# A two-layer decoder trunk: row blocks 4 to 7 first before the up-projections, attention's low parts on VectorE, and three moves in the order of work

## The chip, the cores and the metric

The kernel runs on one core of a Trainium2 chip. A core has a matrix engine (TensorE, PE in the profile; PEld is its weight load), a vector engine (VectorE, DVE), a scalar engine (ScalarE, ACT), a general engine (GpSimd, POOL) and a sync engine (SyncE, SP) that issues DMAs. They run side by side, each in the order of its own instruction stream, and wait for one another by semaphores. On-chip memory is SBUF; matmul results go to PSUM banks. The metric is the device time of one execution in microseconds (us).

## The reference

A trunk of two layers on one sequence of 1024 rows of 1024 numbers (D). Layer 0 mixes rows by a gated linear recurrence (HGRN2, 8 heads), layer 1 by sliding-window attention (window 128, 16 query heads, 4 key/value heads, a learned sink per head, a relative-position bias). Keys and values are projected once, from layer 0's output. After each mixer and after each feed-forward part stands a layer norm with a weighted residual:

```python
for layer in range(DEPTH):
    if layer < N_A_LAYERS:
        mix = hgrn2_mixer(h, hgrn_w_in[layer], ...)
    else:
        mix = swa_sink_mixer(h, k_shared, v_shared, swa_w_q[j], swa_sinks[j], bias, mask, swa_w_out[j])
    h = layer_norm(ALPHA * h + mix, ln_mix_g[layer], ln_mix_b[layer])
    ff = conv_ffn(h, ffn_w_in[layer], ffn_conv_w[layer], ffn_conv_b[layer], ffn_w_out[layer])
    h = layer_norm(ALPHA * h + ff, ln_ffn_g[layer], ln_ffn_b[layer])
    if layer == N_A_LAYERS - 1:
        k_flat, v_flat = jnp.split(h @ shared_w_kv, 2, axis=-1)

def conv_ffn(h, w_in, conv_w, conv_b, w_out):
    u = h @ w_in                       # 1024 -> 2 * 2816
    u = causal_depthwise_conv(u, conv_w, conv_b)     # width 3
    a, b = jnp.split(u, 2, axis=-1)
    return (jax.nn.silu(a) * b) @ w_out

def swa_sink_mixer(...):
    logits = q k^T * dh**-0.5 + bias, masked to the window
    m = max(logits.max(-1), sink);  p = exp(logits - m)
    return (p v / (p.sum(-1) + exp(sink - m))) @ w_out
```

## The kernel before

**Numbers in two parts.** Each matmul operand is held as a high part (a cast to fp32r by ACT, in `split` and `split_into`, L186 and L141) and a low part, source minus high part (L187 and L142, on VectorE, or on GpSimd where the caller asks for it). `mm3` (L159 to L161) makes one product from three matmuls: high by high, high by low, low by high. So PE can start an operand's product when its high part is there, and needs the low parts one and two matmuls later.

**Places.** T holds the transposed activations (both parts), Y the row blocks (8 blocks tb of 128 rows), HL is twelve weight tiles; a pair of them is a slot (`hl_at(i)`, six slots), given out in turn by `ring["hl"]`. `psmm` has four PSUM banks, `psax` two of twice the size.

**Order.** PE's order is that of the program text everywhere; in attention (from the `with tc.manual_schedule` near the end) the order of ACT, VectorE and GpSimd is that of the text too. Elsewhere a scheduler orders the other engines by priority, which follows the text. `Order` (od) is a planner by which chains of small work are put into the text between matmuls: a generator is spawned, yields a waiting time (in us of PE time that the planner counts), and is continued by `od.tick()` when this has passed, or by `od.finish()` at once. Loads go out from SP's queue in the order of its stream.

**Output projection and up-projection** (`out_proj`, `Up`). For each column half dh and each row block tb the projection's product is added to the residual (L321), and half of the norm's statistics taken (L200). In the second half the chain `Up.ln` starts for the block: `ln_normal` (statistics L206, L207, power on GpSimd L208, then the normalisation on VectorE L222 for blocks 0 to 3 or on ACT L218 for blocks 4 to 7), a store of the normal rows (L353), a yield of 8.0, `ln_turn` (eight transposes L169, then the norm's scale and shift out of PSUM, L234 on ACT or L236 on VectorE), and the split into T. The up-projection is done with Strassen-like sums: seven products per group fc of columns (`product`), of which 1 and 2 read rows 0 to 511 of T, 4 and 5 rows 512 to 1023, and 6, 7 and 3 sums of both halves, made by L365 to L369 and held in TX. `weights(fc)` loads a group's weights into the tiles rx and splits them (`weight_load`), then makes sums of them (`weight_sums`, L404 to L407): products 1 and 2 need plain weights, 4 and 5 summed ones. `run` starts with products 1 and 2 of two groups in psax banks, while the chains of blocks 4 to 7 end, then takes products 4 and 5 in psmm banks, and so on.

**From layer 0 to attention.** The down-projection's last evacuations (L578) end blocks 4 to 7. Each block's `ln_mid` normalises, yields 11.0 or 8.0, turns the block through psax banks (two of four columns each on VectorE, L236) and splits it to T. Around these chains PE runs `k_part(0)` (keys of rows 0 to 511; low part Kl on VectorE, L1058), three `v_part`s, `k_part(1)` and the first query projection. Key weights lie in slots 0 and 1, value weights in 2 and 3. `ln_rows` multiplies the normal rows of all eight blocks by the norm's gain (VectorE, L251), adds its shift (GpSimd, L252) and stores them as layer 1's residual; it starts after block 7's chain, during `k_part(1)`.

**Attention.** Eight query groups c, in each four steps bp. A step runs stages of four steps at once: scores (L1119, L1122), copy and mask (L1124 to L1131), bias on GpSimd (L1134), maximum and sink (L1139, L1142, L1143), exponential, division (L1150 to L1152), transposes, triangle mask (L1160), output (L1165 and on), and between them a quarter of the next group's query projection (`q_proj`, `q_split` L1107). Weights of the group after next (`q_unit`) and of the output projection (`out_unit`) and the move of the output from Y to T (`Y_to_T`, steps 26 to 31) have their low parts on GpSimd.

## Time and profile before

| | us |
|---|---|
| median of 3 runs (2301.88 to 2304.33) | 2304.32 |
| profiled execution | 2307.7 |
| its span | 2305.9 |
| PE busy in the span | 2225.4 (97%) |
| DVE busy | 1878.7 (81%) |
| ACT busy | 916.5 (40%) |
| POOL busy | 282.1 (12%) |

The span goes from the first to the last instruction of the profiled execution. Rows of a timeline give start and duration in us, engine, line, operation, tiles and shapes, and in square brackets the idle time before it with what ended it. Rows of a group give busy time and mean duration in ns. A granted clock of 1.00 is TensorE at full speed.

### The profile page before, as it was taken

Reading aid. Unit: us, or ns where it says so; the run is one execution under the profiler, and the core shown is the slowest. Engines: PE = TensorE matmul, PEld = TensorE weight load, DVE = VectorE, ACT = ScalarE, POOL = GpSimd, SP = SyncE. Lnnn points to the kernel's source line nnn. Section 1 sums busy time; section 2 is a strip of 40 time slices with the busy share of each in tenths; the row PEclk is TensorE's granted clock in tenths of the full one; section 3 lists DMA queues with packets and bytes.
Section 4 is the critical chain, followed back from the end, with each engine's and each line's share of the span. In section 5 each row is a group of like instructions: output and inputs, shape, how many; then the busy total and the mean of one; then the engine's idle time right before and its main releaser. Section 6 shows DMA issues by size and latency. Waiting matters only on the chain.

```text
span 2305.9 us, 30677 instructions
## 1 busy us (share of the span) xinstructions
PE 2225.4 (97%) x11743; PEld 1862.0 (81%) x11743; DVE 1878.7 (81%) x2413; ACT 916.5 (40%) x1553; POOL 282.1 (12%) x246
## 2 busy tenths in 40 slices
PE   8999999999989999999999899989999999999998
PEld 7788889888878888888788687767788888887887
DVE  3688887655769988888997658996689888889987
ACT  4122122232555444444343435653744444443431
POOL 0223222221000000000000063450100000000001
PEclk9999999999999999999999999989999999999999
DMA  6355454312312322226955331113212222238663
GB/s 213 39 183 201 165 185 148 95 39 92 110 46 92 101 83 83 83 82 208 306 166 172 93 101 26 41 56 101 92 55 92 92 83 82 83 125 293 217 216 140
DMA packets 231932, 281.32 MB, mean 122 GB/s; under 512 B 29977, under 2 KB 160618, under 8 KB 228970
## 3 DMA queue, kind: packets, MB, share of 16 engines
q1 hardware_dynamic: 228898, 276.92, 36.7%
q10 hardware_dynamic: 2888, 2.45, 0.8%
q8 instruction: 92, 1.51, 0.3%
q14 instruction: 54, 0.44, 0.1%
HBM read 214.31 MB, written 65.01 MB: 121 GB/s over the span
## 4 chain that ended last, share of the span: by engine, by line
PE 70%; DVE 16%; DMA 6%; ACT 4%; issue 3%; POOL 1%; SPq 0%; DVEq 0%; ACTq 0%; POOLq 0%
PE psmm L159 13%; PE psmm L161 13%; PE psmm L160 13%; PE psax L159 8%; PE psax L161 8%; PE psax L160 8%; PE psax L165 4%; DMA raw<-in_hgrn_w_in_dram 2%; DVE T L187 1%; DMA bsd<-Y 1%; ACT Y L234 1%; DVE Y L452 1%; PE psmm L165 1%; DMA Y<-in_ffn_w_out_dram 1%; DVE A L805 1%
## 5 line engine op out<-in xcount | busy, mean ns | idle before, releaser
L159 PE MATMUL psmm<-T,HL 128*128 128x512 f32 x768 | 311.4, 406 | 5.6 <-ACT T L186 5.6
L160 PE MATMUL psmm<-T,HL 128*128 128x512 f32 x768 | 303.8, 396 | 4.9 <-DVE T L187 4.9
L161 PE MATMUL psmm<-T,HL 128*128 128x512 f32 x768 | 304.3, 396 | 4.0 <-DVE HL L142 4.0
L452 DVE SCALAR_TENSOR_TENSOR Y<-Y,cwt 128x1023 f32<-128x1023 f32 (+1 forms) x176 | 225.0, 1279 | 40.6 <-ACT Y L450 40.3
L450 ACT ACTIVATE Y<-Y,cwt 128x1024 f32<-128x1024 f32 x88 | 108.9, 1238 | 269.2 <-DVE Y L439 265.1
L159 PE MATMUL psmm<-HL,T 128*128 128x256 f32 (+1 forms) x656 | 199.3, 304 | 1.8 <-issue 1.4
L161 PE MATMUL psmm<-HL,T 128*128 128x256 f32 (+1 forms) x656 | 195.6, 298 | 1.0 <-DVE T L187 1.0
L160 PE MATMUL psmm<-HL,T 128*128 128x256 f32 (+1 forms) x656 | 195.6, 298 | 0.6 <-DVE HL L142 0.6
L208 POOL TENSOR_TENSOR rs<-rs,nhalf 128x1 f32<-128x1 f32 x32 | 26.4, 826 | 1375.8 <-DVE rs L207 1375.6
L186 ACT CAST HL<-rx 128x1024 fp32r<-128x1024 f32 (+1 forms) x137 | 140.3, 1045 | 130.6 <-DMA rx<-in_ffn_w_in_dram 44.8
L161 PEld LDWEIGHTS psmm<-T,HL 128*128 128x128 f32 x768 | 146.6, 191 | 36.8 <-DVE HL L142 4.5
L187 DVE TENSOR_TENSOR HL<-rx,HL 128x1024 fp32r<-128x1024 f32 (+1 forms) x137 | 165.2, 1210 | 13.5 <-ACT HL L186 13.2
L159 PEld LDWEIGHTS psmm<-T,HL 128*128 128x128 f32 x768 | 147.0, 191 | 36.0 <-ACT T L186 6.5
L160 PEld LDWEIGHTS psmm<-T,HL 128*128 128x128 f32 x768 | 146.9, 191 | 34.3 <-DVE T L187 5.5
L159 PE MATMUL psax<-T,HL 128*128 128x512 f32 x352 | 137.9, 392 | 0.0
L161 PE MATMUL psax<-T,HL 128*128 128x512 f32 x352 | 137.4, 390 | 0.0
L160 PE MATMUL psax<-T,HL 128*128 128x512 f32 x352 | 137.1, 389 | 0.0
L159 PEld LDWEIGHTS psmm<-HL,T 128*128 128x128 f32 x656 | 126.8, 193 | 5.7 <-issue 1.6
L160 PEld LDWEIGHTS psmm<-HL,T 128*128 128x128 f32 x656 | 126.6, 193 | 4.5 <-DVE HL L142 0.9
L161 PEld LDWEIGHTS psmm<-HL,T 128*128 128x128 f32 x656 | 126.2, 192 | 4.6 <-DVE T L187 1.2
L825 POOL TENSOR_TENSOR kp<-kp,tot 128x512 f32<-128x512 f32 x48 | 69.3, 1443 | 216.8 <-PE psax L165 182.9
L186 ACT CAST HT<-rx 128x1024 fp32r<-128x1024 f32 (+1 forms) x51 | 43.9, 861 | 95.8 <-PE psmm L160 30.1
(301 smaller groups left out, 5547.4 us busy)
## 6 DMA issues: line engine op xcount, KB each, us to landing
rx<-in_ffn_w_in_dram SPq DMA_DIRECT2D x136, 256.0 KB, 3.4
rx<-gd SPq DMA_DIRECT2D x118, 256.0 KB, 3.4
Y<-in_ffn_w_out_dram SPq DMA_DIRECT2D x44, 512.0 KB, 3.7
bsd<-Y SPq DMA_DIRECT2D x22, 1024.0 KB, 7.2
gd<-Y SPq DMA_DIRECT2D x44, 512.0 KB, 2.7
rx<-in_ffn_w_out_dram SPq DMA_DIRECT2D x54, 256.0 KB, 3.9
R<-bsd SPq DMA_DIRECT2D x44, 256.0 KB, 4.4
Y<-in_ffn_w_in_dram SPq DMA_DIRECT2D x40, 256.0 KB, 3.0
```

Of the source, the lines that this page charges most:

```text
L159: nc.tensor.matmul(ps, st(0), mv(0), start=start, stop=False)
L160: nc.tensor.matmul(ps, st(0), mv(1), start=False, stop=False)
L161: nc.tensor.matmul(ps, st(1), mv(0), start=False, stop=stop)
L165: nc.tensor.matmul(ps, lhsT, rhs, start=start, stop=stop, **kw)
L186: nc.scalar.copy(hi, src)
L187: return (eng or nc.vector).tensor_tensor(lo, src, hi.bitcast(F32), op=ALU.subtract)
L208: nc.gpsimd.tensor_tensor(rs, rs, nhalf, op=ALU.pow)
L234: nc.scalar.activation(hf[:, kc, :], ps[:, k * P:(k + 1) * P], AF.Identity, bias=shift, scale=scale)
L450: nc.scalar.activation(c, u, AF.Identity, bias=cwt[:, l, 3, ci:ci + 1], scale=cwt[:, l, 2, ci:ci + 1])
L452: nc.vector.scalar_tensor_tensor(c[:, sh:], u[:, :S - sh], cwt[:, l, 2 - sh, ci:ci + 1], c[:, sh:], op0=ALU.mult, op1=ALU.add)
L805: nc.vector.copy_predicated(dst, mask.unsqueeze(1).to_broadcast(list(dst.shape)), src)
L825: nc.gpsimd.tensor_tensor(kv[:, :, 0, :], kv[:, :, 0, :], tv[:, :, 1:2].to_broadcast([P, nb, m]), op=ALU.mult)
```

## The change

Five parts:

- `out_proj` takes the row blocks of its second column half in the order 4, 5, 6, 7, 0, 1, 2, 3. The up-projection begins with products 4 and 5 of two groups (psax banks); when the last chains are done, products 1 and 2 follow in psmm banks. Sums of both halves are now made in the chains of blocks 0 to 3. Blocks 2 and 3 are turned into rx[1] and rx[2].
- `urgent()`, a raised priority for the scheduler, stands around the evacuation and the norm's chain in `out_proj` and `Up.ln`.
- Key weights go to slots 4 and 5, value weights to 0 and 1; query and output weights get slots from a written list.
- `ln_mid` waits 9.0 instead of 8.0 for blocks 4 to 7 and turns a block in two halves with a yield of 1.2 between them. `ln_rows` runs in two batches: blocks 0 to 3 are spawned before `k_part(0)`, blocks 4 to 7 where all eight were.
- The low parts of query weights, output weights and `Y_to_T` go to a list, `lows`, and are issued on VectorE: late in each attention step, after `q_split`, and for the first two query units right after their casts.

```diff
@@ -120,6 +120,10 @@
     def psax():
         return axp.tile([P, 1024], F32, name="psax")
 
+    def urgent():
+
+        return tc.high_priority(offset=300)
+
 
     ring = {"hl": 4, "raw": 0}
     tail, place = {}, {}
@@ -137,9 +141,17 @@
             nc.sync.dma_start(view, src)
         return raw
 
+    def low_part(lo, src, hi, eng):
+
+        make = lambda e: e.tensor_tensor(lo, src, hi.bitcast(F32), op=ALU.subtract)
+        if isinstance(eng, list):
+            eng.append(lambda: make(nc.vector))
+        else:
+            return make(eng or nc.vector)
+
     def split_into(hl, raw, eng=None):
         nc.scalar.copy(hl[:, 0], raw)
-        (eng or nc.vector).tensor_tensor(hl[:, 1], raw, hl[:, 0].bitcast(F32), op=ALU.subtract)
+        low_part(hl[:, 1], raw, hl[:, 0], eng)
         return hl
 
     def split_raw(raw, eng=None):
@@ -184,7 +196,7 @@
 
     def split(hi, lo, src, eng=None):
         nc.scalar.copy(hi, src)
-        return (eng or nc.vector).tensor_tensor(lo, src, hi.bitcast(F32), op=ALU.subtract)
+        return low_part(lo, src, hi, eng)
 
     def split_scaled(hi, lo, src, scale):
         nc.scalar.activation(hi, src, AF.Copy, scale=scale)
@@ -221,9 +233,9 @@
             yq = y[:, q * 512:(q + 1) * 512]
             nc.vector.tensor_scalar(yq, yq, mv[:, 0:1], rs, op0=ALU.subtract, op1=ALU.mult)
 
-    def ln_turn(tb, hf, gcol, bcol, banks, on_vector=0):
-
-        for q in range(2):
+    def ln_turn(tb, hf, gcol, bcol, banks, on_vector=0, halves=range(2)):
+
+        for q in halves:
             ps = banks(q)
             for k in range(4):
                 tr(ps[:, k * P:(k + 1) * P], Y[:, tb, (4 * q + k) * P:(4 * q + k + 1) * P])
@@ -238,20 +250,22 @@
 
     def ln_mid(tb, gcol, bcol):
         ln_normal(tb)
-        yield 11.0 if tb < 4 else 8.0
+        yield 11.0 if tb < 4 else 9.0
         hf = place["hf"](tb)
-        ln_turn(tb, hf, gcol, bcol, lambda q: psax()[:, :512], 2)
+        for q in range(2):
+            ln_turn(tb, hf, gcol, bcol, lambda _: psax()[:, :512], 2, (q,))
+            if q == 0:
+                yield 1.2
         ts = slice(tb * P, (tb + 1) * P)
         split(T[:, 0, :, ts], T[:, 1, :, ts], hf)
 
-    def ln_rows(rows, wait, spill=None):
-        for tb in range(NB):
+    def ln_rows(tbs, rows, wait, spill):
+        for tb in tbs:
             for h in range(2):
                 y = Y[:, tb, h * 512:(h + 1) * 512]
                 nc.vector.tensor_tensor(y, y, rows[0][h], op=ALU.mult)
                 nc.gpsimd.tensor_tensor(y, y, rows[1][h], op=ALU.add)
-            if spill is not None:
-                nc.sync.dma_start(spill[:, tb, :], Y[:, tb, :])
+            nc.sync.dma_start(spill[:, tb, :], Y[:, tb, :])
             yield wait
 
     def ln_last(tb, rows):
@@ -312,14 +326,17 @@
                     out_late(late, rows, tb, ff.TX)
                 elif dh == 0 and tb == 4:
                     ff.weights(0)
+                if dh:
+                    tb = (tb + 4) % NB
                 if dh == 0 and tb < len(begun):
                     ps = begun[tb]
                 else:
                     ps = psmm()
                     out_part(ps, late if dh else us, tb, range(KC))
                 y = Y[:, tb, dh * 512:(dh + 1) * 512]
-                nc.vector.scalar_tensor_tensor(y, y, ALPHA, ps, op0=ALU.mult, op1=ALU.add)
-                ln_half(tb, dh)
+                with urgent() if dh else nullcontext():
+                    nc.vector.scalar_tensor_tensor(y, y, ALPHA, ps, op0=ALU.mult, op1=ALU.add)
+                    ln_half(tb, dh)
                 if dh == 1:
                     tasks.append(od.spawn(ln(tb)))
                     od.tick()
@@ -349,28 +366,31 @@
             self.W, self.raw, self.pieces = {}, {}, 0
 
         def ln(self, tb, gcol, bcol):
-            ln_normal(tb, tb > 3)
-            nc.sync.dma_start(ynd[:, tb, :], Y[:, tb, :])
+            with urgent():
+                ln_normal(tb, tb > 3)
+                nc.sync.dma_start(ynd[:, tb, :], Y[:, tb, :])
             yield 8.0
-            turned = lambda t: (self.rx[2] if t == NB - 1 else Y[:, t, :]).rearrange("p (k t) -> p k t", k=KC)
+            turned = lambda t: (self.rx[t - 1] if t in (2, 3) else Y[:, t, :]).rearrange("p (k t) -> p k t", k=KC)
             hf = turned(tb)
-            ln_turn(tb, hf, gcol, bcol, lambda q: psmm())
             ts = slice(tb * P, (tb + 1) * P)
-            if tb < 4:
+            with urgent():
+                ln_turn(tb, hf, gcol, bcol, lambda q: psmm())
+                if tb > 3:
+                    a21, a22 = hf[:, :4], hf[:, 4:]
+                    split(T[:, 0, 4:, ts], T[:, 1, 4:, ts], a22)
+                    tt(a22, a21, a22, op=add)
+                    split(T[:, 0, :4, ts], T[:, 1, :4, ts], a22)
+                    return
                 split(T[:, 0, :, ts], T[:, 1, :, ts], hf)
-                return
-            pf, xs = turned(tb - 4), slice((tb - 4) * P, (tb - 3) * P)
-            a11, a12, a21, a22 = pf[:, :4], pf[:, 4:], hf[:, :4], hf[:, 4:]
-            split(T[:, 0, 4:, ts], T[:, 1, 4:, ts], a22)
-            tt(a22, a21, a22, op=add)
-            split(T[:, 0, :4, ts], T[:, 1, :4, ts], a22)
+            sf = turned(tb + 4)
+            a11, a12, a21, s1 = hf[:, :4], hf[:, 4:], sf[:, :4], sf[:, 4:]
             tt(a21, a11, a21, op=sub)
-            tt(a11, a22, a11, op=sub)
+            tt(a11, s1, a11, op=sub)
             tt(a12, a12, a11, op=sub)
-            split(self.TX[:, 2, 0, :, xs], self.TX[:, 2, 1, :, xs], a21)
+            split(self.TX[:, 2, 0, :, ts], self.TX[:, 2, 1, :, ts], a21)
             yield 100.0
-            pair = pf.rearrange("p (c k) t -> p c k t", c=2)
-            split(self.TX[:, :2, 0, :, xs], self.TX[:, :2, 1, :, xs], pair)
+            pair = hf.rearrange("p (c k) t -> p c k t", c=2)
+            split(self.TX[:, :2, 0, :, ts], self.TX[:, :2, 1, :, ts], pair)
 
         def weights(self, fc):
             self.weight_load(fc)
@@ -458,26 +478,24 @@
                     nc.sync.dma_start(gd[:, fc, :], ca)
 
         def run(self, ready, down):
+
             od.finish(ready[:4])
             tiles = [psax(), psax()]
             ax = [tiles[i % 2][:, i // 2 * 512:(i // 2 + 1) * 512] for i in range(4)]
-            first = [(p, fc) for fc in range(2) for p in (1, 2)]
-            for (p, fc), ps in zip(first, ax):
+
+            for (p, fc), ps in zip([(p, fc) for p in (4, 5) for fc in range(2)], ax):
                 self.product(p, fc, ps)
             od.finish(ready[4:])
             mm = [psmm() for _ in range(4)]
             self.pairs = [mm, ax]
-            for (p, fc), ps in zip(first, ax):
-                self.collect(p, fc, ps)
-
-            for n, (p, fc) in enumerate([(p, fc) for p in (4, 5) for fc in range(2)]):
-                self.product(p, fc, mm[n])
+            for (p, fc), ps in zip([(p, fc) for p in (1, 2) for fc in range(2)], mm):
+                self.collect(p, fc, self.product(p, fc, ps))
             for fc in range(2):
-                self.collect(6, fc, self.product(6, fc, ax[fc]))
+                self.collect(6, fc, self.product(6, fc, mm[fc]))
             for fc in range(2):
-                self.collect(7, fc, self.product(7, fc, ax[2 + fc]))
-                self.collect(4, fc, mm[fc])
-                self.collect(5, fc, mm[2 + fc])
+                self.collect(7, fc, self.product(7, fc, mm[2 + fc]))
+                self.collect(4, fc, ax[fc])
+                self.collect(5, fc, ax[2 + fc])
             self.weight_load(2)
             for fc in range(2):
                 self.product(3, fc, mm[fc])
@@ -1038,14 +1056,14 @@
         Vt = at.tile([P, NB, 256], F32, name="Vt")
         khl, uv = [], []
         for c in range(2):
-            hl = split_into(hl_at(c), load(lambda r: [(r.rearrange("p (k c) -> p k c", k=KC),
+            hl = split_into(hl_at(4 + c), load(lambda r: [(r.rearrange("p (k c) -> p k c", k=KC),
                                                        wkvv[:, :, c * P:(c + 1) * P])]))
             khl.append(hl.rearrange("p h (k c) -> p h k c", k=KC))
         for u in range(2):
-            hl = split_into(hl_at(2 + u), load(lambda r: [(r.rearrange("p (k c) -> p k c", k=4),
+            hl = split_into(hl_at(u), load(lambda r: [(r.rearrange("p (k c) -> p k c", k=4),
                                                            wkvv[:, 4 * u:4 * u + 4, 256:512])]))
             uv.append(hl.rearrange("p h (k c) -> p h k c", k=4))
-        ring["hl"] = 4
+
         def k_part(half):
             ts = slice(half * 512, (half + 1) * 512)
             for c in range(2):
@@ -1077,11 +1095,14 @@
             nc.sync.dma_start(bfs[c], bass.AP(tensor=rbd.tensor, offset=rbd.offset + (8 * pp + r) * 2 * P * P + P - 1,
                                               ap=[[2 * P - 1, P], [8 * P * P, 2], [1, P]]))
 
+        lows = []
+
         def q_unit(c):
             bias_load(c)
             pp, r = divmod(c, 4)
+            ring["hl"] = (2, 3, 4, 5, 0, 1, 4, 5)[c]
             hl = unit(lambda t: [(t.rearrange("p (k g e) -> p k g e", k=KC, g=2)[:, :, g, :],
-                                  wq[:, :, 8 * pp + 4 * g + r, :]) for g in range(2)], nc.gpsimd)
+                                  wq[:, :, 8 * pp + 4 * g + r, :]) for g in range(2)], lows)
             return hl.rearrange("p h (k c) -> p h k c", k=KC)
 
         def q_proj(hl):
@@ -1204,25 +1225,32 @@
             out_part(begun[1], us, 1, [6])
             yield
 
+        def make_lows():
+            while lows:
+                lows.pop(0)()
+
         flight = []
         with tc.manual_schedule(engines={EN.PE, EN.Activation, EN.DVE, EN.Pool}):
             od.finish(lns[:4])
+            late = [od.spawn(ln_rows(range(4), rows, 2.0, h2d))]
             k_part(0)
             for tp in range(3):
                 od.finish(lns[2 * tp:2 * tp + 2])
                 v_part(tp)
             od.finish(lns[6:])
             hl = q_unit(0)
-            late = od.spawn(ln_rows(rows, 2.0, h2d))
+            make_lows()
+            late.append(od.spawn(ln_rows(range(4, NB), rows, 2.0, h2d)))
             k_part(1)
             g = q_proj(hl)
             q, done = next(g)
             hl = q_unit(1)
+            make_lows()
             for _ in g:
                 while done:
                     q_split(*done.pop(0))
                 od.tick()
-            od.finish([late])
+            od.finish(late)
             nc.scalar.activation(sm.tile([P, 1], F32, name="warm"), nhalf, AF.Exp)
             us = []
             moves = {26: (0, 3, 0, 4), 27: (3, 6, 0, 4), 28: (0, 3, 4, 8), 29: (3, 6, 4, 8),
@@ -1235,7 +1263,7 @@
                     it = attend(c, bp, q)
                     prev = [None] * (3 - len(flight)) + flight
                     if 4 * c + bp in moves:
-                        Y_to_T(*moves[4 * c + bp], nc.gpsimd)
+                        Y_to_T(*moves[4 * c + bp], lows)
                     stage(it)
                     stage(prev[0])
                     stage(prev[2])
@@ -1246,6 +1274,7 @@
                     stage(prev[2])
                     while done:
                         q_split(*done.pop(0))
+                    make_lows()
                     if bp == 0 and c < 6:
                         hl = q_unit(c + 2)
                     stage(fill)
@@ -1256,7 +1285,8 @@
                     if c == 0 and bp == 1:
                         v_part(3)
                     if 0 <= 4 * c + bp - 21 < 4:
-                        us.extend(out_unit(rows2, 4 * c + bp - 21, nc.gpsimd))
+                        ring["hl"] = 4 * c + bp - 21
+                        us.extend(out_unit(rows2, 4 * c + bp - 21, lows))
                     flight.append(it)
                 q = nq
             a29, a30, a31 = flight
```

2 lines of the change are left out of this document (1 added, 1 removed).

## The prediction

> **What bounds the kernel now.** I read the busy times first, then windows over the stretches where TensorE (PE) has gaps, then PE's waits there, and last the timelines of the engine that ended each wait.
>
> ```profile
> span 2305.9 us, 30677 instructions
> ## 1 busy us (share of the span) xinstructions
> PE 2225.4 (97%) x11743; PEld 1862.0 (81%) x11743; DVE 1878.7 (81%) x2413; ACT 916.5 (40%) x1553; POOL 282.1 (12%) x246
> ```
>
> PE is busy 97%, and the change leaves its matmuls what they are. So only PE's idle time, 2305.9 − 2225.4 = 80.5 us, and stretches at a lowered clock can be won, or added to. The profiled run took 2307.7 us, 3.4 above the median of 2304.32; I sum against it and carry the difference over to the median.
>
> ```profile
> 643.50:663.50 20.00, 14.12 (x68) 10.81 (x67) 16.75 (x28) 18.28 (x38) 2.23 (x5) 0.98 0.22 79
> 663.50:677.20 13.70, 13.70 (x49) 11.04 (x50) 10.66 (x14) 5.22 (x8) 0.00 (x0) 0.79 0.13 38
> 1296.50:1321.00 24.50, 17.55 (x83) 13.28 (x82) 17.89 (x33) 11.87 (x21) 1.10 (x2) 0.93 0.40 86
> 1378.50:1384.00 5.50, 5.43 (x20) 4.28 (x21) 4.69 (x11) 2.82 (x11) 1.49 (x2) 0.69 0.06 9
> 1400.00:1500.00 100.00, 99.74 (x695) 78.79 (x694) 88.38 (x177) 61.07 (x218) 41.03 (x48) 1.00 0.15 38
> 1501.80:1564.50 62.70, 51.70 (x324) 39.61 (x323) 57.83 (x95) 34.70 (x111) 36.14 (x24) 0.89 0.17 59
> ```
>
> Columns: window, length, busy time of PE, weight load, VectorE (DVE), ScalarE (ACT) and GpSimd (POOL), granted clock, DMA share, GB/s. In attention's middle (1400 to 1500) PE is full. It is not in four places that the change touches: the start of each up-projection (A), the hand-over from layer 0 to the key projection (B), attention's start (C) and its end (D).
>
> **A: the first products, both layers.** Before, products 1 and 2 run on row blocks 0 to 3, and product 4 then waits for block 7.
>
> ```profile
> 653.20 1.03 PE L169 MATMUL psmm<-ident,Y 128*128 128x128 f32 x8
> ...
> 660.37 0.50 PE L159 MATMUL psmm<-T,HL 128*128 128x512 f32 x1 [2.70 <-ACT T L186]
> 663.30 0.80 PE L160 MATMUL psmm<-T,HL 128*128 128x512 f32 x1 [2.43 <-DVE T L187]
> ```
> ```profile
> 1667.64 0.50 PE L159 MATMUL psmm<-T,HL 128*128 128x512 f32 x1 [2.94 <-ACT T L186]
> 1670.57 0.80 PE L160 MATMUL psmm<-T,HL 128*128 128x512 f32 x1 [2.43 <-DVE T L187]
> ```
> ```profile
> 654.91 1.05 ACT L186 CAST HL<-rx 128x1024 fp32r<-128x1024 f32 x1
> 655.85 0.64 ACT L186 CAST T<-Y 128x512 fp32r<-128x512 f32 x1
> 656.37 2.92 ACT L234 ACTIVATE rx<-psmm,par 128x128 f32<-128x128 f32 x8
> 659.12 0.68 ACT L186 CAST T<-Y 128x512 fp32r<-128x512 f32 x1
> 659.63 0.69 ACT L186 CAST T<-rx 128x512 fp32r<-128x512 f32 x1
> ```
> ```profile
> 661.36 0.68 DVE L187 TENSOR_TENSOR TX<-Y,TX 128x512 fp32r<-128x512 f32 x1
> 661.96 0.68 DVE L369 TENSOR_TENSOR Y<-Y 128x512 f32<-128x512 f32 x1
> 662.56 0.68 DVE L187 TENSOR_TENSOR T<-rx,T 128x512 fp32r<-128x512 f32 x1
> ```
>
> Block 7's turn on ACT begins at 656.37, three microseconds behind its transposes, since a weight cast (HL<-rx) and block 6's cast stand ahead of it and it needs rx[2], which that cast has to read first. Its low part stands behind sums of block 6 (TX, L369). The idle is 2.70 + 2.43 = 5.1 us, and the clock behind it falls to 0.79 over 13.7 us, 0.21 × 13.7 = 2.9 us: 8.0 in layer 0; in layer 1, 2.94 + 2.43 and as much clock, 8.3.
>
> After, blocks 4 to 7 come first in the second column half, products 4 and 5 run on them, and products 1 and 2 wait for block 3, whose chain now ends last. Products 4 and 5 need the weight sums of both first groups; these stand on DVE some 20 us ahead of the products in the new order. I keep the end of block 3's transposes at block 7's (653.20, first rows just after). Its eight turns take 2.92 and no longer wait for rx[2] (block 3 goes to rx[2] too, which the weight sums, now earlier, have left by then), so they end near 656; one cast of 1024 columns at 1.05 and one low part (below, 1.22) follow, to 657.3 and 658.4. PE comes off products 4 and 5 when it came off the first products, at 660.37 − 2.70 = 657.7, or up to 0.8 earlier: waits of about 0.4 and 0.9 us, and I add 0.8 of clock, 2.1 in all. The gain is 5.9 and 6.2, **−12.1**. It is at least 3.5 (should the TX cast and two sums get ahead of it, 1.6 + 2 × 0.68 a layer, with the whole clock loss kept) and at most 16.3, all of it. The loads that are moved (the next weights' on SP's queue behind the products, four 128 KB pieces) are due after some 20 us; sums pushed back by the urgent evacuations are due at product 6, four products later, which take the 13.7 us of the second window. I cost both at nothing; without that cover product 6 would wait by one pair of sums, 1.4 us.
>
> **B: layer 0's end, key projection.**
>
> ```profile
> PE psmm L161 <- DVE HL L142: 4.0, 1, 4.0
> PE psax L169 <- DVE q L236: 2.6, 2, 2.3
> PE psax L169 <- issue: 0.3, 1, 0.3
> ```
> ```profile
> L236 DVE TENSOR_SCALAR q<-psax,par 128x128 f32<-128x128 f32 x16 | 5.6, 404 | 1.5 <-ACT q L234 1.5
> L1058 DVE TENSOR_TENSOR Kl<-psmm,Kh 64x512 fp32r<-64x512 f32 x8 | 5.5, 687 | 18.0 <-ACT Kh L1057 17.9
> L187 DVE TENSOR_TENSOR T<-q,T 128x1024 fp32r<-128x1024 f32 x4 | 4.9, 1225 | 4.7 <-ACT T L186 4.7
> L142 DVE TENSOR_TENSOR HL<-raw,HL 128x1024 fp32r<-128x1024 f32 x4 | 4.8, 1216 | 0.3 <-ACT HL L141 0.3
> ```
> ```profile
> 1288.61 0.69 DVE L578 TENSOR_TENSOR Y<-Y,psmm 128x512 f32<-128x512 f32 x1 [6.62 <-PE psmm L161]
> ```
> ```profile
> L251 DVE TENSOR_TENSOR Y<-Y,X 128x512 f32<-128x512 f32 x16 | 18.0, 1185 | 0.1
> ```
>
> (PE's waits from 1296 to 1322; groups from 1296 to 1580, the last two numbers before the bar being busy us and mean ns.) The key weights' slots 0 and 1 come free only with the down-projection's end, hence the wait of 4.0 us for their low part. In slots 4 and 5 the two low parts (2 × 1.22) fit into DVE's idle 6.62 us before 1288.61, so the 4.0 go. Against it stands the first batch of residual rows: eight multiplications on DVE, 8 × 1.185 = 9.5 us, each followed by an addition on POOL, put between the norm of blocks 4 to 7 and the turns (L236) that release PE's two transpose banks. DVE's window has 17.89 of 24.5 busy; without the four lows and with the rows it is 17.89 − 4.8 + 9.5 = 22.6, and PE can run ahead of nothing: it owns two banks, and the turn in two halves makes it come back for each. Placing the instructions in the new order by these durations, PE stalls 5.4 us for the first turn (behind block 7's norm and the first pair of rows), 1.7 and 2.3 at the next, and 6.2 behind a low part, Kl's four casts and more rows: 15.6 in place of 4.0 + 2.6 + 0.3 = 6.9, with 1.2 less of clock lost. **+7.5**; from −3 (rows hidden in the free 6.6 us) to +11 (all 9.5 uncovered, and one more turn). The four stores of residual rows move up SP's queue with them, ahead of the query weights' loads; those are due some 20 us later.
>
> **C: attention's start.**
>
> ```profile
> 1361.52 0.33 PE L1119 MATMUL psax<-Kh,q 128*128 128x128 f32 x1 [1.02 <-DVE q L1107]
> ```
> ```profile
> 1378.57 0.63 PE L169 MATMUL psmm<-ident,X 128*128 128x128 f32 x4 [1.45 <-DVE X L1152]
> ```
> ```profile
> 1358.82 12.25 POOL L252 TENSOR_TENSOR Y<-Y,X 128x512 f32<-128x512 f32 x8
> ```
>
> POOL's backlog of rows lasts until 1371 and holds up the first bias additions; PE idles 1.02 and 1.45 and then runs at 0.69 for 5.5 us (1.7): 4.2 us. With half of the rows gone and the low parts of two query units on DVE I leave 0.4: **−3.8** (0 if those lows delay DVE as much; −5 at best).
>
> The Trainium skill (TensorE: Matmul & The Clock Gate, "Why this matters for your kernels") asks for no PE gaps over some 3 us, since one idle window lowers the clock. The trace differs: the gap of 1.45 us has a clock of 0.69 right behind it. By the page the small waits left in A would cost no clock, and the sum would be 1.6 us lower; I go by the trace.
>
> **D: attention's end.**
>
> ```profile
> 1529.67 0.16 DVE L1142 SCALAR_TENSOR_TENSOR nm<-nm,nsk 128x4 f32<-128x4 f32 x1
> 1529.87 3.39 DVE L1143 TENSOR_TENSOR se<-sk,nm 128x4 f32<-128x4 f32 x1
> ```
> ```profile
> 1529.79 3.45 POOL L187 TENSOR_TENSOR T<-Y,T 128x1536 fp32r<-128x1536 f32 x1 [3.90 <-ACT T L186]
> ```
>
> A DVE instruction on four columns takes 3.39 us, as long as the POOL low part beside it, where its like took 0.16: DVE stands still while POOL reads. In the window PE idles 62.7 − 51.7 = 11.0 us and loses 0.11 × 51.7 = 5.7 to the clock: 16.7. After, the lows are DVE's own: five of 1.22, four 1536 wide at 1.5 × 1.22 = 1.83, two 512 wide at 0.68, 14.8 us in eleven steps, put last in each step, where nothing of that step waits behind them. Bounds: all hidden but for DVE's leftover share, 11.6% of 62.7 = 7.3, would leave 14.8 − 7.3 = 7.5 if that share is all there is, none if the freed stalls count too (−13 after some lost clock); nothing hidden leaves 14.8 (−2). I leave 8.0, near the row of the free share: **−8.7**. The casts stand a step ahead of the lows, so DVE does not wait for them.
>
> The Trainium skill (SBUF — State Buffer, "Who interferes with whom") says that a DVE instruction with two SBUF inputs and a GpSimd instruction that reads SBUF lock each other out wholly. The rows of D agree, and it speaks against B, where such pairs are moved into the norm's window; the mean of 1185 ns has that lock in it.
>
> **Sum:** −12.1 + 7.5 − 3.8 − 8.7 = −17.1: 2307.7 − 17.1 = 2290.6 for the profiled run, 2304.3 − 17.1 = **2287** for the median.
>
> **Rivals.** (1) B is hidden: rows fit into DVE's gaps and the 4.0 is won. For it: DVE's 6.6 free us; against: two banks only. 2304.3 − 12.1 − 3 − 3.8 − 8.7 = 2277. (2) A brings nothing: block 3 ends as late against PE as block 7 did, for the same casts and sums still stand on ACT and DVE, and the urgent order moves only some. Against: one cast of 1024 replaces two steps and a sum. 2304.3 + 7.5 − 3.8 − 8.7 = 2299. (3) Slower: DVE becomes attention's bound. If none of its free time can be used and the stalls remain for another reason, the lows of all attention, 12 × 1.22 + 4 × 1.83 + 2 × 0.68 = 23.3 us, are added with none of D won: 2304.3 − 12.1 + 7.5 − 3.8 + 23.3 = 2319. It decides once attention gets longer by 8.4 us. For it: DVE at 88.38% while PE is full; against: that share includes its standing still beside POOL.
>
> **How the numbers follow.** Likeliest 0.54, around 2287 (2280 to 2296 by itself); (1) 0.17; (2) 0.15, about half of it within 0.2% (4.6 us, about what can be told from no change); (3) 0.14, a tenth of it inside that bound. Faster is 0.54 + 0.17 + 0.08 = 0.79, same 0.08, slower 0.13. The range takes in (1) and (2): 2274 to 2301, and leaves out (3) and the tail under (1).
>
> **What would show it.** Right: PE's waits for T at the first products under 1 us each, with the clock above 0.9 behind them; no wait for HL in the first key matmul; L236 late and longer PE waits on psax from 1300 to 1330; L1142 and L1143 at 0.16 throughout, steps of the last two query groups between 5.6 and 6.8 us. Wrong: the wait at product 1 as long as product 4's was; attention's middle with PE below 97 of 100 us; or a new wait on slots of HL.

## The result and the profile after

The changed kernel takes 2293.71 us (median of 5 runs, 2293.41 to 2294.85), the kernel before 2304.33 beside it: a ratio of 0.9951, 95% interval 0.9937 to 0.9966, 10.6 us less. The forecast was 2287, 17.1 us less.

The page after, and a table of windows over the four places (length, busy time of PE, weight load, DVE, ACT and POOL, granted clock, DMA share, GB/s): the first products of layer 0 (A), the hand-over to the key projection (B), attention's start (C) and its end (D).

```profile
span 2291.7 us, 30675 instructions
...
PE 2221.3 (97%) x11743; PEld 1861.2 (81%) x11743; DVE 1866.8 (81%) x2431; ACT 917.0 (40%) x1553; POOL 237.0 (10%) x228
```
```profile
657.00:675.00 18.00, 15.08 (x59) 11.71 (x58) 10.59 (x14) 7.81 (x10) 0.00 (x0) 0.91 0.30 87
1293.00:1328.00 35.00, 22.38 (x101) 18.12 (x100) 26.04 (x44) 13.79 (x26) 13.03 (x10) 0.80 0.34 96
1364.00:1372.00 8.00, 7.43 (x36) 5.50 (x35) 3.65 (x9) 5.42 (x9) 1.88 (x4) 1.00 0.31 66
1497.00:1549.50 52.50, 50.20 (x334) 38.98 (x333) 48.11 (x95) 35.33 (x106) 12.86 (x14) 0.97 0.19 62
```

The window of D is now 52.5 us long with PE busy for 50.2 of them, where it was 62.7 with 51.7 (334 PE instructions against 324). B has become the worst place: 35 us with 22.4 busy, at a clock of 0.80. DVE has the low parts and yet less busy time in the span than before (1866.8 against 1878.7): in attention's last steps it no longer stands still beside GpSimd.

Every trace holds the same 11743 PE instructions (matmuls and transposes), so a stretch can be taken between the same two PE instructions, counted in PE's order, in two traces. The table gives how much longer (+) or shorter (−) each stretch is than in the first profile of before, in us: A0 and A1 the up-projections' starts in layers 0 and 1 (593.7 to 735.8 and 1640.6 to 1761.1 before), B 1284.1 to 1323.9, C 1343.0 to 1399.5, D 1486.5 to 1598.6, and the rest of the span. The times are medians; the ratio is to the kernel before, run beside it on the same chip.

| run | A0 | B | C | D | A1 | rest | us | ratio, interval |
|---|---|---|---|---|---|---|---|---|
| changed | −5.5 | +8.3 | −3.8 | −10.4 | −4.1 | +1.3 | 2293.71 | 0.9951, 0.9937 to 0.9966 |
| before_again | −1.0 | +1.0 | −1.6 | 0.0 | +0.3 | +2.0 | 2306.82 | 1.0001, 0.9989 to 1.0013 |
| rows_once | −5.5 | +3.6 | +4.0 | −10.4 | −5.9 | +4.2 | 2295.51 | 0.9961, 0.9946 to 0.9976 |
| turn_whole | −4.8 | +3.8 | −3.8 | −10.4 | −4.0 | +2.2 | 2290.60 | 0.9931, 0.9910 to 0.9951 |
| rows_once_whole | −4.1 | −2.9 | +4.1 | −10.4 | −5.8 | +8.4 | 2290.88 | 0.9936, 0.9915 to 0.9956 |
| pool_lows | −4.5 | +8.9 | −3.8 | 0.0 | −4.3 | +1.3 | 2304.26 | 0.9998, 0.9988 to 1.0007 |
| order_back | +0.5 | +9.3 | −3.8 | −10.2 | −0.1 | −2.0 | 2301.14 | 0.9984, 0.9974 to 0.9993 |
| slots_back | −5.3 | +11.4 | −3.8 | −10.4 | −3.9 | +3.5 | 2298.11 | 0.9959, 0.9942 to 0.9977 |
| cast_half | −9.1 | +7.7 | −3.8 | −10.4 | −8.2 | +3.5 | 2286.86 | 0.9910, 0.9893 to 0.9927 |
| rows_v_whole | −4.3 | +6.1 | −3.7 | −10.4 | −3.2 | +2.0 | 2294.21 | 0.9942, 0.9926 to 0.9959 |
| best | −9.2 | +6.2 | −3.3 | −10.3 | −7.7 | +3.4 | 2287.25 | 0.9914, 0.9894 to 0.9935 |
| best2 | −8.7 | −5.7 | +3.2 | −10.3 | −7.9 | +5.6 | 2279.75 | 0.9884, 0.9866 to 0.9903 |
| best3 | −8.7 | −6.3 | +7.4 | −10.3 | −8.1 | +0.8 | 2283.64 | 0.9902, 0.9885 to 0.9920 |

The rest holds little that was changed: attention's middle, 1399.5 to 1486.5, where low parts moved too, is 0.4 us shorter in every run but pool_lows and before_again. Yet the rest goes from −2 to +8 us from profile to profile. Most of that lies in the first 165 us, where every engine has the same instructions in the same order in all fourteen traces, and which still take from 0.6 us less to 5.6 us more than in the first profile. So a time says less of a part than the stretch that the part touches. Stretches that a run leaves alone repeat better: D within 0.2 us, C within 0.1 but for the two profiles of before, B from +7.7 to +9.3, A1 from −3.2 to −5.9. The last section shows that the lowered clock comes in steps of some 1.7 us, and A1 had none, one or two of them.

### The profile page after: what moved, and what is told of

Read it like the earlier page. It is cut to its first block, busy times and chain, and to the rows that moved or that the text cites. A ratio compares the mean times of both kernels' runs of the same rounds, so it can differ in the third digit from the quotient of the medians.

```text
span 2291.7 us, 30675 instructions
## 1 busy us (share of the span) xinstructions
PE 2221.3 (97%) x11743; PEld 1861.2 (81%) x11743; DVE 1866.8 (81%) x2431; ACT 917.0 (40%) x1553; POOL 237.0 (10%) x228
## 5 line engine op out<-in xcount | busy, mean ns | idle before, releaser
L146 DVE TENSOR_TENSOR HL<-raw,HL 128x1024 fp32r<-128x1024 f32 x51 | 66.9, 1314 | 48.2 <-ACT HL L153 48.1
```

The lines of the kernel that those rows point to most:

```text
L146: make = lambda e: e.tensor_tensor(lo, src, hi.bitcast(F32), op=ALU.subtract)
```

## The experiments

**The kernel before once more.** 

> The kernel before, once more, for a second profile. If the 3.4 us by which its first profile was longer than the median of its runs lie in stretches that the change does not touch (the first 600 us), the stretches of this profile differ from the first by 1 to 3 us there and by less than 0.5 us from the first up-projection on; then the gain of the four places is taken from them, and not from the difference of the two profiled times. If they lie in the four places, the gains read there were too large.

The second profile has stretches from the first up-projection on that differ by up to 1.6 us, not by less than 0.5, and its run is again longer than its median (2308.55 against 2306.82). In the four places, first and second profile differ by just over 1 us in sum. So the gains read from the table are good to one or two microseconds each; the sum of the changed kernel's places, −15.5, and the measured −10.6 are not reconciled by it.

**Attention's low parts back on GpSimd.**

```diff
-for g in range(2)], lows)                      # q_unit
+for g in range(2)], lows if c < 2 else nc.gpsimd)
-Y_to_T(*moves[4 * c + bp], lows)
+Y_to_T(*moves[4 * c + bp], nc.gpsimd)
-us.extend(out_unit(rows2, 4 * c + bp - 21, lows))
+us.extend(out_unit(rows2, 4 * c + bp - 21, nc.gpsimd))
```

> Low parts of attention's steps back on GpSimd (the first two query units' stay on VectorE), all else as changed. Theory: attention's last eleven steps lost their time to VectorE standing still beside GpSimd's low parts; its small instructions take 1.6 to 3.4 us again there, the stretch is about 10.9 us longer, 2304 us. Rival: the new order of slots and the later place of the lows did it; then within 2 us of 2294.

D is back at 0.0, 10.4 us longer than in the changed kernel, at 2304.26. Groups of DVE from attention's part of each trace (the last two numbers before the bar are busy us and mean ns), first of this run, then of the changed kernel:

```profile
L1163 DVE SCALAR_TENSOR_TENSOR nm<-nm,nsk 128x4 f32<-128x4 f32 x32 | 26.0, 811 | 1.1
```
```profile
L1163 DVE SCALAR_TENSOR_TENSOR nm<-nm,nsk 128x4 f32<-128x4 f32 x32 | 5.2, 162 | 1.1
```

The same four-column instruction takes 0.81 us on average with the low parts on GpSimd and 0.16 without: over 32 of them 21 us of DVE. A timeline of DVE in this run shows that it is not one operation's doing: here this instruction takes 0.17 us and the next, also of four columns, 3.37, as in the kernel before. GpSimd's low part of 1536 columns runs beside it:

```profile
1530.53 0.17 DVE L1163 SCALAR_TENSOR_TENSOR nm<-nm,nsk 128x4 f32<-128x4 f32 x1
1530.73 3.37 DVE L1164 TENSOR_TENSOR se<-sk,nm 128x4 f32<-128x4 f32 x1
```
```profile
1530.64 3.45 POOL L146 TENSOR_TENSOR T<-Y,T 128x1536 fp32r<-128x1536 f32 x1 [3.89 <-ACT T L198]
```

That D's gain comes from taking the low parts off GpSimd, and not from the slots, is shown. This run also gives up their later place in the step, and no run puts them at another place on DVE; what the place is worth by itself is not shown.

**The row blocks' order back.**

```diff
-                if dh:
-                    tb = (tb + 4) % NB
...
-            for (p, fc), ps in zip([(p, fc) for p in (4, 5) for fc in range(2)], ax):
+            first = [(p, fc) for fc in range(2) for p in (1, 2)]
+            for (p, fc), ps in zip(first, ax):
```

(and the bodies of `Up.ln` and `run` that go with it, with `urgent()` kept)

> Row blocks in the order 0 to 7 and products 1 and 2 first as before, the raised priority and all else as changed. Theory: the order won the 5.5 and 3.7 us at the two up-projections, so both come back: PE waits for block 7's T by 2.7 + 2.4 us again, 2303 us. Rival: the raised priority alone won them: waits under 3.5 us in sum per layer, 2294 to 2297 us.

A0 and A1 are at +0.5 and −0.1: without the order (and the places of blocks 2 and 3 that belong to it), the raised priority wins nothing that shows, and the time is 2301.14. PE's timeline in this run:

```profile
662.48 0.62 PE L171 MATMUL psmm<-T,HL 128*128 128x512 f32 x1 [3.56 <-ACT T L198]
663.69 0.80 PE L172 MATMUL psmm<-T,HL 128*128 128x512 f32 x1 [0.60 <-DVE T L146]
```

The waits came in another division than expected (3.6 + 0.6, not 2.7 + 2.4), with two shorter ones, 0.39 and 1.54 us for the norm on ACT, ahead of them.

**What is left at the first products.** PE, ACT and DVE of the changed kernel at layer 0's first product, and PE in layer 1:

```profile
659.87 0.51 PE L171 MATMUL psmm<-T,HL 128*128 128x512 f32 x1 [2.17 <-ACT T L198]
661.13 0.69 PE L172 MATMUL psmm<-T,HL 128*128 128x512 f32 x1 [0.75 <-DVE T L146]
```
```profile
1656.94 0.50 PE L171 MATMUL psmm<-T,HL 128*128 128x512 f32 x1 [2.17 <-ACT T L198]
1658.20 0.80 PE L172 MATMUL psmm<-T,HL 128*128 128x512 f32 x1 [0.76 <-DVE T L146]
```
```profile
658.25 0.62 ACT L198 CAST TX<-Y 128x512 fp32r<-128x512 f32 x1 [1.37 <-DVE Y L387]
658.78 1.04 ACT L198 CAST T<-rx 128x1024 fp32r<-128x1024 f32 x1
```
```profile
656.21 0.68 DVE L388 TENSOR_TENSOR rx<-Y,rx 128x512 f32<-128x512 f32 x1
656.93 0.69 DVE L389 TENSOR_TENSOR rx<-rx 128x512 f32<-128x512 f32 x1
657.54 0.68 DVE L387 TENSOR_TENSOR Y<-rx,Y 128x512 f32<-128x512 f32 x1
```

Block 3's cast to T was ready when its turn ended (1.37 us before 658.25), but stands on ACT behind a cast of TX, and that one waits for a sum on DVE, behind two sums of block 2. The next run splits the turn:

```diff
-                ln_turn(tb, hf, gcol, bcol, lambda q: psmm())
-                split(T[:, 0, :, ts], T[:, 1, :, ts], hf)
+                    for q in range(2):
+                        ln_turn(tb, hf, gcol, bcol, lambda _: psmm(), halves=(q,))
+                        qs = slice(4 * q, 4 * q + 4)
+                        split(T[:, 0, qs, ts], T[:, 1, qs, ts], hf[:, qs])
```

> As changed, but blocks 0 to 3 are turned and split to T in two halves before the up-projections, so that product 1 needs only the first half. Theory: the 2.2 + 0.75 us left at product 1 are there because block 3's cast to T stands on ScalarE behind a cast of TX that waits for VectorE's sums; with a first half that needs neither, both waits go below 0.5 us and with the clock 3 to 4 us are won in each layer: 2287 us. Rival: the chain of block 3 is late by its norm and turn; then the waits stay above 2 us and the time within 2 us of 2294.

2286.86 us, with A0 and A1 3.6 and 4.1 us shorter still. One wait of 1.3 us is left in each layer, for the first half's low part, not under 0.5; the clock behind it is full:

```profile
659.95 0.50 PE L172 MATMUL psmm<-T,HL 128*128 128x512 f32 x1 [1.27 <-DVE T L146]
```
```profile
659.00:675.00 16.00, 15.05 (x66) 12.39 (x67) 12.34 (x17) 7.29 (x10) 0.00 (x0) 1.00 0.35 99
```

**B: rows, halves and slots.** PE's waits in the changed kernel between the down-projection's end and the value products (us in total, times, longest):

```profile
PE psax L181 <- DVE q L248: 7.2, 2, 5.0
PE psax L181 <- ACT q L246: 5.4, 1, 5.4
```

Three runs take it apart. The first has all rows in one batch after block 7's turn:

```diff
-            late = [od.spawn(ln_rows(range(4), rows, 2.0, h2d))]
+            late = []
...
-            late.append(od.spawn(ln_rows(range(4, NB), rows, 2.0, h2d)))
+            late.append(od.spawn(ln_rows(range(NB), rows, 2.0, h2d)))
```

> Theory: the eight multiplications of residual rows that stand on VectorE between the turns of blocks 4 to 7 hold PE's two transpose banks. With all rows after block 7's turn, PE's three waits for psax there (5.0 + 2.2 + 5.4 = 12.6 us in the changed kernel) fall under 5 us, this stretch is 8 us shorter, and the start of attention gets back the 3.8 us that it had gained: about 2290 us. Rival: it is the turn in two halves with its longer yield that leaves PE waiting; then the three waits stay near 12 us and the time goes up by the 3.8 us, to 2297.

B got 4.7 us shorter, not 8, and C lost 7.8, not 3.8; 2295.51. The waits in B and C:

```profile
PE psax L181 <- ACT q L246: 5.1, 1, 5.1
PE psax L181 <- DVE q L248: 3.7, 1, 3.7
```
```profile
PE psax L1140 <- DVE q L1128: 4.7, 2, 3.8
```

So neither theory holds as it stood: rows are a part of B's loss, the 5.1 us for ACT are not theirs, and the first batch earns in C more than it costs in B. The second run has the turn in one go:

```diff
-        yield 11.0 if tb < 4 else 9.0
+        yield 11.0 if tb < 4 else 8.0
-        for q in range(2):
-            ln_turn(tb, hf, gcol, bcol, lambda _: psax()[:, :512], 2, (q,))
-            if q == 0:
-                yield 1.2
+        ln_turn(tb, hf, gcol, bcol, lambda q: psax()[:, :512], 2)
```

> All of the changed kernel but the norm's turn in one go after 8.0, as before. Theory (rows are the cause): PE's waits for psax stay above 9 us in sum and the time is within 3 us of the changed kernel's, 2291 to 2297. Rival (the halves are the cause): they fall under 4 us and the time to 2285.

The waits stayed at 11.2 us in sum (9.7 and 1.5), as the theory had it, and yet B is 4.5 us shorter. Of these only 1.4 are waits. The others are clock: counted as half of PE's busy time while the trace's clock stood at 0.50, B loses 1.6 us to it here and 5.2 in the changed kernel, since most of the time at 0.50 fell into the long wait, where PE had nothing to do. That wait has another cause here: with the other order of turns the second key weight's load went out behind the norm's gain and shift rows, and its low part stopped DVE ahead of block 4's norm:

```profile
1290.36 1.05 ACT L153 CAST HL<-raw 128x1024 fp32r<-128x1024 f32 x1 [7.35 <-DMA raw<-in_shared_w_kv_dram]
```
```profile
1291.44 1.23 DVE L146 TENSOR_TENSOR HL<-raw,HL 128x1024 fp32r<-128x1024 f32 x1 [3.81 <-ACT HL L153]
1292.59 0.20 DVE L218 BATCH_NORM_AGGREGATE mv<-st 128x2 f32<-128x12 f32 x1
```

So this run moved a load as well and doesn't price the halves alone. The third run does both, whole turns for blocks 4 to 7 alone, so that the load keeps its place:

```diff
-        yield 11.0 if tb < 4 else 9.0
+        yield 11.0 if tb < 4 else 8.0
...
-            if q == 0:
+            if q == 0 and tb < 4:
...
-            late = [od.spawn(ln_rows(range(4), rows, 2.0, h2d))]
+            late = []
```

> As changed, but residual rows in one batch after block 7's turn and the turn of blocks 4 to 7 in one go after 8.0 (blocks 0 to 3 stay in halves, so that the key weights' loads keep their place on the sync engine's queue). Theory: the rows and the halves each cost about 4.5 us between the down-projection's end and the value products, at different waits (the first three at the turn of blocks 4 and 5, the last one of 5 us at block 6, where ScalarE's turn stands behind the key casts); without both, the stretch is 8 to 10 us shorter than in the changed kernel, while attention's start loses the 7.8 us that the first batch had saved there: 2292 us. Rival: one wait in two places; then the stretch stays as in either run alone, 4 to 5 us shorter, and the time is 2297.

B is 11.2 us shorter than in the changed kernel, and C 7.9 longer: the theory, with 2290.88. One wait is left in B:

```profile
PE psax L181 <- DVE q L248: 5.1, 1, 5.1
```

From rows_once to this run only the halves and their longer yields go, and B is 6.5 us shorter: 3.7 of waits, the one for ACT among them, and some 3 of clock (4.4 to 1.5 us). So in this order rows are worth 4.7 us and halves 6.5, 11.2 together. Whether the halves would be worth less with the rows left in, as the 4.5 us of turn_whole suggest, is open. The slots alone:

```diff
-            hl = split_into(hl_at(4 + c), load(...
+            hl = split_into(hl_at(c), load(...
-            hl = split_into(hl_at(u), load(...
+            hl = split_into(hl_at(2 + u), load(...
-            ring["hl"] = (2, 3, 4, 5, 0, 1, 4, 5)[c]
+            ring["hl"] = (4, 5, 0, 1, 2, 3, 4, 5)[c]
```

> Key weights in slots 0 and 1 again, value weights in 2 and 3, query weights in the order of before; all else as changed. Theory of the prediction: the 4.0 us wait for the key weights' low part comes back in full, 2298 us. Rival: in the changed order PE waits 5.0 us for psax at that place anyway, and the two waits overlap; then the sum of the waits from the down-projection's end to the value products grows by less than 2 us, 2294 to 2296 us.

```profile
PE psax L181 <- ACT q L246: 5.4, 1, 5.4
PE psax L181 <- DVE q L248: 4.5, 3, 2.1
PE psmm L173 <- DVE HL L146: 3.7, 1, 3.7
```

The wait for the low part is back with 3.7 us, and 2.7 of the 7.2 us for L248 went into it. So the sum of the waits grew by only 1.0 us, to 13.6, as the rival had it. B is 3.1 us longer even so, since the clock takes 7.0 us there in place of 5.2. The time, 2298.11, is what the theory said, but for another reason; against the kernel before, beside each, it is 7.5 us less where the changed kernel's was 10.6.

**Rows beside the value products.** DVE is idle there, as a window of the changed kernel shows (1.35 of 17 us busy):

```profile
1328.00:1345.00 17.00, 17.00 (x136) 16.63 (x135) 1.35 (x3) 4.46 (x7) 0.00 (x0) 1.00 0.00 1
```

So the next runs put all rows behind the turns and ahead of the value products, and the value weights' low parts behind turns (the first of them with the turn in one go, by the edit of turn_whole):

```diff
-            late = [od.spawn(ln_rows(range(4), rows, 2.0, h2d))]
             k_part(0)
+            od.finish(lns[4:])
+            late = [od.spawn(ln_rows(range(NB), rows, 2.0, h2d))]
...
+        if tb > 5:
+            lows.pop(0)()                      # at the end of ln_mid
```

> As changed, but the turn in one go after 8.0, the value weights' low parts behind the turns of blocks 6 and 7, and all residual rows in one batch after them, beside the value products, where VectorE was idle for 14 us. Theory (both the rows and the place of small work on VectorE ahead of the turns made the loss): PE's waits from the down-projection's end to the value products fall to under 5 us, this stretch is 8 to 11 us shorter than in the changed kernel, attention's start keeps its gain: 2284 us. Rival: the wait is set by block 7's norm itself; then the stretch is as in the run with the turn in one go, 2290 us.

2294.21: a miss. B is only 2.2 us shorter; the load's order is that of the run with whole turns (6.5 us for L248), and PE waits 5.9 us for a value weight's low part, which stands behind block 7's turn. With the half casts:

> The two edits before this one together (half casts, and rows beside the value products with the turn in one go). If they do not touch each other their gains add: 2278 us; if the shorter up-projection start is given back elsewhere, 2284.

2287.25, no better than the half casts alone. Then whole turns for blocks 4 to 7 only, block 4's wholly on ACT, and the value weights' low parts behind blocks 5 and 6:

```diff
+            ln_turn(tb, hf, gcol, bcol, lambda _: psax()[:, :512], 0 if tb == 4 else 2, (q,))
+            if q == 0 and tb < 4:
...
+        if tb in (5, 6):
+            lows.pop(0)()
```

> Half casts at the up-projections; turn in halves for blocks 0 to 3 and whole for 4 to 7, block 4's wholly on ScalarE; value weights' low parts behind the turns of blocks 5 and 6; all residual rows beside the value products. Theory: with the rows, the value weights and the halves out of VectorE's way, PE's waits from the down-projection's end to the value products fall from 12.6 us to under 4, attention's start keeps its gain and the up-projections win 3.6 and 4.1 us more than the changed kernel: 2275 to 2279 us. Rival: value products wait for their weights' low part again as they did with these behind blocks 6 and 7; then 2282 to 2286.

2279.75 us, ratio 0.9884 to before: the shortest of this study, though its interval overlaps with those of cast_half and best3. B is 14.0 us shorter than in the changed kernel and its waits sum to 3.1 us at a clock of 1.00. But C went from −3.8 to +3.2, against the theory. Waits in B and C, and the clock from 1292 to 1325:

```profile
PE psax L181 <- issue: 1.4, 1, 1.4
PE psax L181 <- DVE q L248: 1.0, 1, 1.0
PE psax L181 <- ACT q L246: 0.7, 1, 0.7
```
```profile
PE psmm L173 <- DVE HL L146: 4.4, 1, 4.4
```
```profile
1292.00:1325.00 33.00, 29.84 (x196) 26.16 (x195) 23.75 (x40) 19.04 (x36) 4.12 (x5) 1.00 0.21 45
```

The 4.4 us are for the first query unit's low part, behind fourteen multiplications of rows on DVE. The last run moves it ahead of them:

```diff
             od.finish(lns[4:])
+            hl = q_unit(0)
+            make_lows()
             late = [od.spawn(ln_rows(range(NB), rows, 2.0, h2d))]
...
-            hl = q_unit(0)
-            make_lows()
```

> As the run before with half casts and all rows beside the value products, but the first query unit's low part ahead of the rows on VectorE and not behind fourteen of them. Theory: the rows take 1.74 us each in step with GpSimd's additions, so they end where attention starts, and the 4.4 us that PE waited there for this low part (with the clock behind it) go: the stretch from the key part to attention's start is 6 to 7 us shorter, 2273 us. Rival: the rows then delay the low parts of the second half's keys and PE waits for them at the first scores instead: 2278 to 2280 us.

The rival came out, and more than it said: C is at +7.4, 2283.64. The wait moved to the first scores, and the groups of DVE and POOL from 1296 to 1360 tell why (the last row is another addition of the same size on POOL, without such a neighbour):

```profile
1353.53 0.48 PE L1146 MATMUL psax<-Kh,q 128*128 128x128 f32 x1 [7.95 <-DVE q L1134]
```
```profile
L270 DVE TENSOR_TENSOR Y<-Y,X 128x512 f32<-128x512 f32 x16 | 25.1, 1643 | 0.0
```
```profile
L271 POOL TENSOR_TENSOR Y<-Y,X 128x512 f32<-128x512 f32 x16 | 26.7, 1708 | 25.7 <-DVE Y L270 25.7
```
```profile
L1161 POOL TENSOR_TENSOR X<-X,bf 128x512 f32<-128x512 f32 x1 | 1.3, 1285 | 0.1
```

Sixteen pairs in a row go at 1.7 us a pair on both engines, 27 us in all, and the value products last 17. What stands behind them on DVE is late: the low parts of the second half's keys, then the second query unit's, then the query's split, for which PE waits. Two batches, one beside the value products and one behind the keys, were not tried.

## The prediction, step by step

**A, −12.1 forecast, −9.6 measured** (−5.5 and −4.1; against the mean of both profiles of before 0.3 us less). The order does it, as order_back shows. PE came off products 4 and 5 at 657.7, as worked out. The size was off on the other side: "waits of about 0.4 and 0.9 us, and I add 0.8 of clock" came out as 2.17, 0.75 and, by the clock records, 1.7, because the TX cast and the sums got ahead of block 3's cast, which had been given as the lower end only. cast_half measures that step: 7.7 us in both layers. By this alone layer 0 would have gained 3.4 us, not 5.5; the difference is mostly shorter waits ahead of these products (1.1 us where there had been 2.4), which the sum did not have: luck. The lower end itself, 3.5, does not come out of its terms: 1.6 + 2 × 0.68 us more of waits and 2.9 of clock in each layer leave about 2.

**B, +7.5 forecast, +8.3 measured.** The sum held, its parts did not. The waits were 12.6 us, not 15.6: 5.0 for 5.4 at the first turn, 2.2 for 1.7 + 2.3, and 5.4 for 6.2. In their place the clock fell to 0.80 over 35 us, 0.20 × 22.38 busy = 4.5 us (5.2 by the clock records), where the prediction had all of the 1.2 us of before going away. That the two errors nearly cancel is luck. And the last of the waits was put down to rows as well: it goes with the halves and their yields, since rows_once keeps 5.1 of it and rows_once_whole none. There, block 6's turn on ACT stands behind the key casts. The 4.0 us counted as won by the new slots were not won as such: slots_back shows 1.0 us of waits and 1.8 of clock.

**C, −3.8 forecast, −3.8 measured**; one wait of 0.57 us is left. The second profile of before is 1.6 us shorter there than the first, so that the gain is 2.2 to 3.8: the 1.7 us of clock in the forecast were in one profile and not in the other. rows_once, at +4.0, shows that the first batch of rows wins C; the query units' low parts were not tried by themselves there.

**D, −8.7 forecast, −10.4 measured**, within its bounds of 2 to 13. The step that was too careful is "I leave 8.0": over the whole of D the changed kernel has 3.7 us without work for PE and loses 1.7 to the clock, 5.4. So DVE's freed stalls counted too, and not its free share alone.

**The whole.** The rest of the span is 1.3 us longer in the changed profile, where nothing was forecast, and the difference of the medians, 10.6 us, is smaller than that of the profiled runs, 2307.7 − 2293.5 = 14.2: the first profile of before was an execution longer than the median, the changed one was not. The four places' −15.5 lie just outside the interval (−7.8 to −14.5), with the rest, −14.2, just inside. Of the 3.6 us between −14.2 and −10.6, some 1.7 can be the clock in C, which the second profile of before does not lose; where the others lie is not settled, and the first 165 us alone vary by more. The rivals fell: B was not hidden, A brought something, and attention's middle stayed the same (−0.4 us from 1399.5 to 1486.5), so DVE did not become its bound.

The lock that the Trainium skill gives for two-input VectorE instructions beside GpSimd reads (SBUF — State Buffer, "Who interferes with whom") showed on both sides: D won 10.4 us by leaving it, and the rows pay for it at 1.7 us a pair. That is more than GpSimd's 1.28 us alone and less than the 1.96 of 1.28 and VectorE's 0.68 one behind the other, so in the rows the two are not kept apart for the whole of both instructions.

## What to carry to other kernels

An operation of little cost on an idle engine can hold up a full one, if the two share a way to memory: look for instructions whose duration does not go with their size (here four columns in 3.4 us). When a piece of work is moved between engines or earlier in an in-order queue, ask of every instruction behind it who waits for it; the residual rows cost 4.7 us at one place and 7.8 at another, and the 17 us beside the value products did not hold their 27. A wait's price is its length and the clock behind it: turn_whole won 4.5 us with 1.4 us less of waits, and slots_back lost 3.1 with 1.0 us more. So compare whole stretches between the same two instructions, and not sums of waits.

## What had not been expected of the hardware

The clock behind a short gap is not set by the gap's length alone. In the first profile of before a gap of 1.45 us was followed by a clock of 0.69; in the second profile of the same kernel the same gap, 1.43 us, was followed by full speed:

```profile
1381.12 0.41 PE L169 MATMUL psmm<-ident,X 128*128 128x128 f32 x2 [1.43 <-DVE X L1152]
```
```profile
1381.10:1386.60 5.50, 5.48 (x37) 4.31 (x37) 4.69 (x11) 3.21 (x12) 1.50 (x2) 1.00 0.06 10
```

In the changed kernel a gap of 1.30 us at attention's end had 0.66 behind it, and in cast_half the one of 1.27 us shown above had 1.00:

```profile
1528.15 2.15 PE L177 MATMUL psmm<-W,Vt 128*64 128x128 f32 x14 [1.30 <-DVE W L1181]
```
```profile
1528.00:1533.00 5.00, 4.85 (x26) 3.91 (x27) 4.86 (x12) 3.12 (x9) 2.63 (x3) 0.66 0.00 0
```

So a wait under 2 us may or may not cost some 1.7 us more, and two profiles of one kernel differ by that. The trace's clock records show how. In all fourteen traces the granted clock is 1.00 or 0.50 and nothing between, and it stays at 0.50 for 3.41 us or a whole multiple of it (but for the end of the execution), along a grid of 3.41 us steps that lies differently in each execution; 0.66, 0.69 or 0.80 are means over a longer window. One step at 0.50 costs a busy PE half of it, 1.7 us. Two neighbouring steps of this grid at each gap (columns as in the table of windows), first in the first profile of before, then in the second:

```profile
1376.00:1379.40 3.40, 1.95 (x13) 1.47 (x13) 2.11 (x7) 2.24 (x10) 1.39 (x2) 0.99 0.75 154
1379.40:1382.80 3.40, 3.40 (x10) 2.63 (x9) 3.29 (x8) 2.13 (x10) 1.38 (x2) 0.50 0.00 0
```
```profile
1377.40:1380.80 3.40, 2.29 (x17) 1.68 (x15) 2.15 (x6) 2.69 (x11) 1.97 (x3) 1.00 0.53 120
1380.80:1384.20 3.40, 3.08 (x16) 2.65 (x17) 3.28 (x10) 2.24 (x10) 1.50 (x2) 1.00 0.22 36
```

In the first the gap lies in one step, which is left 57% busy, and the next is at half speed; in the second it is divided between two steps, and none is. Over the fourteen traces (without the first 21 us and the end from 2270), of 89 full-speed steps in which PE was busy for less than half, 88 had a step at 0.50 behind them; of 171 between half and 0.7 it was 20, and of the 8789 above that, none. So a wait that empties over half of a step cost the next step's speed here, and a wait of 1.0 to 1.7 us may do so, more likely when it falls into one step. Within that range chance is left: the gap of 1.30 us left its step 62% busy and was followed by 0.50, the one of 1.27 us left 63% and was followed by 1.00.

So the 0.8 us of clock that the prediction had in each layer of A can hardly come as such: it is none or about 1.7. The waits of 2.17 and 0.75 us lost 1.7 and 1.6, and the 1.27 us of cast_half none.
